# Order of TensorE's products in the column-chunk part of a decoder block: y, combining, transpose and gate products in program order

## The chip, the cores and the metric

The kernel runs on one core of a Trainium2 chip. The metric is the device time of one execution in microseconds. A core has five engines with a queue of instructions each: TensorE (PE in the profile) multiplies matrices into PSUM, VectorE (DVE) and ScalarE (ACT) work on tiles in SBUF and PSUM, GpSimd (POOL) does little here, and SyncE (SP) issues nearly all transfers. Sixteen DMA engines carry these out. An engine takes its instructions in the order of its queue; between engines semaphores order the work.

## The reference

One layer of a decoder block on 256 tokens of width 2048, all in fp32: a recurrent and a convolutional mixer share one input and one output projection; a mixture of 32 experts follows, and a gated embedding:

```
x = x + concat(o_hg, o_sc) @ w_out
hn = rms_norm(x, g_ffn)
x = x + hier_moe(hn, ...)            # one group of 4, two experts of 8; w_gate, w_up, w_down of 32 experts
ple = rms_norm(p @ w_ple, g_ple)
x = x + sigmoid(x @ w_ple_gate) * ple
return rms_norm(x, g_final)
```

An expert computes `(silu(a) * b) @ w_down[e]` with `a = xb @ w_gate[e]` and `b = xb @ w_up[e]`. Its three matrices are 2048x512, 2048x512 and 512x2048, 4 MB each, so 32 experts bring 384 MB through the core, and `w_ple_gate` (2048x2048) 16 MB.

## The kernel before, in words

The tokens are kept as two halves j = 0, 1 of 128 rows. The residual stream is `x1[j]` (128 x 2048). Experts go in eight blocks b = 0..7 of four. Each expert takes up to 32 tokens, so the four experts of a block are put side by side on the array: a product of expert e uses a strip of 32 columns of the array (shown as 128*32), and four experts fill the 128 columns.

After the gate and up products of all blocks (`hT`, the hidden values, transposed), the down products come in two parts. In the first (L1042 to L1060, blocks 0 to 3, `NBR = 4`) whole rows of `w_down` are loaded. In the second, the column-chunk part (L1141 to L1193, blocks 4 to 7), the 2048 output columns are taken in five chunks, `CHUNKS` of 512, 512, 512, 256 and 256 columns; all four blocks are done for one chunk before the next starts. By numbers: chunk 0 to chunk 4. The reason for chunks is that a finished chunk of the residual stream lets the product `x @ w_ple_gate` begin for these rows.

In a chunk, for each block b: four weight pieces (two in the chunks of 256 columns, where a piece holds two experts) are taken from the list of loaded ones; 16 products (4 parts f of the hidden width, 4 experts e) give `ys`, 128 slots x w, in PSUM (L1162); the slots of the weights are refilled, that is, the next piece on the list is issued into them; ScalarE copies `ys` to `yt` (L1171). `combine` (L1150) multiplies with `PwT[b]`, which spreads the slots to the tokens with their weights, and adds into `acc[j]`. It is called one block late: combine(b-1) after y(b), and combine(7) at the end of the chunk.

A fp32 product stands as two instructions in the trace; a gate product (fp32r) and a transpose as one.

When a chunk is done, its gate work becomes a generator, `embedding_gate`, which the next chunk advances by `next(job)`: `residual` adds `acc` to `x1` on VectorE (L1080), transposes the chunk on TensorE (L1087) and splits it to a high and a low part (ScalarE L1089, VectorE L1090). For each of four column groups n, `split_gate` splits the gate weights in the same way (ScalarE L1102, VectorE L1103, into two slots that are used in turn), and `gate_mm` (L1112 to L1114) multiplies, three products for each k and half j: 24 products per n for a chunk of 512, 12 for 256. The sum over chunks, `Gs`, is kept in SBUF (L1137, L1139). In the last chunk `gate_sum` (L1121) puts a part of `Gs` back into PSUM, and after the last combine the gate of chunk 4 itself ends the kernel with the sigmoid, the final norm and the stores.

The generator is advanced twice in the first block of a chunk (`residual` and the first split; then gate group 0 and the next split), once in each other block, and twice in the second block of chunk 4.

Weights come in pieces of 1 MB through SP's queue in one fixed list; in this part for each chunk: the pieces of block 4, half of the gate pieces of the chunk before, block 5, the other half, block 6, block 7. Ten slots are in turn in this part: a piece is issued when the slot ten pieces back is free.

The order of the instructions on an engine is not the order of the Python lines. A scheduler at compile time simulates the program and takes what it believes to be ready; it may move a product of y between gate products, or a combine ahead of a gate group. `tc.issue_after(ins)` gives each instruction of its block an edge behind `ins` on the same engine: it fixes the order and adds no semaphore. Before the change only two places near the end use it in this part (L1196, L1223).

PSUM: four banks `mm` (the accumulators, later the sums of the gate) and four banks `ms` that go round between y, x2T and G.

Of the kernel before, what the change touches and what calls it, by code (L numbers as in the profile page):

```python
# [15 lines left out]
P = 128  # L16
# [10 lines left out]
NB = NE // 4  # L27
CAP = 32
B_PLE = NB - 4
NBR = NB - 4  # L30
# [5 lines left out]
def kernel(ctx, tc, a, out, dbg=None):  # L36
    nc = tc.nc
# [14 lines left out]
    def slot(i, shape, dt=F32, name="t"):  # L52
        return slots.tile(shape, dt, tag=f"s{i}", name=nm(name))

    def tmp4(shape, name="tmp"):
        return tmp.tile(shape, F32, tag="tmp", name=nm(name))

    def bank(shape=(P, 512), name="mm"):
        return psA.tile(list(shape), F32, tag="mm", name=nm(name))

    def misc(shape=(P, 512), name="ms"):
        return psB.tile(list(shape), F32, tag="ms", name=nm(name))

    def f32(t):
        return t.bitcast(F32)

    V, A, G, MM = nc.vector, nc.scalar, nc.gpsimd, nc.tensor.matmul
# [3 lines left out]
    ident = consts[:, 0:P]  # L71
# [81 lines left out]
    state = {"next": 0}  # L153
# [12 lines left out]
    def take():  # L166
        return loaded.pop(0)
# [43 lines left out]
    ps = misc(name="vg")  # L211
# [99 lines left out]
    def refill_slot(s):  # L311
        if want[0] > 0:
            want[0] -= 1
            free.append(s)
        elif state["next"] < limit.get(s, 1 << 30):
            give(s)
# [208 lines left out]
    ps = misc((P, 4, 4), "gf")  # L525
# [104 lines left out]
    x1 = []  # L630
# [136 lines left out]
    ps = misc((P, P), "cntT")  # L767
# [9 lines left out]
    hT, ple = [], []  # L777
# [153 lines left out]
    for b in range(NB):  # L931
# [7 lines left out]
        if b == 0:  # L939
# [3 lines left out]
            hT = [slot(free.pop(0), [P, 2, NB, P], name="hT") for _ in range(2)]  # L943
        if b == B_PLE:
            ple = [slot(free.pop(0), [P, D], name="ple") for _ in range(2)]
            PwT = slot(free.pop(0), [P, NB, T], name="PwT")
# [96 lines left out]
    for b in range(NBR):  # L1043
        ys = [bank(name="y") for _ in range(4)]
        for k in range(4):
            four = [take() for _ in range(4)]
            for n in range(4):
                for e in range(4):
                    q = slice(32 * e, 32 * e + 32)
# [14 lines left out]
    Gs = [slot(xg_slots[j], [P, D], name="G") for j in range(2)]  # L1064
    want[0] += 3
    gate_slots = []

    def accumulator(w):

        if w == 512:  # L1070
            return [bank(name="acc") for _ in range(2)], 1
        t = bank((P, 2, w), "acc")
        return [t[:, j] for j in range(2)], 2

    def residual(c0, w, acc):

        nk = w // P
        cs = slice(c0, c0 + w)
        for j in range(2):
            V.tensor_tensor(x1[j][:, cs], acc[j], x1[j][:, cs], OP.add)  # L1080
        t = slot(xt_slot, [P, 2, 4, T], F32R, name="x2T")
        for k2 in range(0, nk, 2):
            ps = misc((P, 2, T), "x2T")
            for kk in range(2):
                k = c0 // P + k2 + kk
                for j in range(2):
                    state["x2T"] = nc.tensor.transpose(ps[:, kk, j * P:(j + 1) * P], x1[j][:, k * P:(k + 1) * P], ident)  # L1087
            ks = slice(k2, k2 + 2)
            A.copy(t[:, 0, ks], ps)  # L1089
            V.tensor_tensor(t[:, 1, ks], ps, f32(t[:, 0, ks]), OP.subtract)  # L1090
        return t

    def split_gate(n, mine, slots_):

        c = (n % 2) * 512
        part = []
        for i, g in enumerate(mine):
            s = slots_.pop(0)
            slots_.append(s)
            t = slot(s, [P, 2, 2, 512], F32R, name="ghl")  # L1100
            src = g[1][:, :, c:c + 512]
            state["split"] = A.copy(t[:, 0], src)  # L1102
            V.tensor_tensor(t[:, 1], src, f32(t[:, 0]), OP.subtract)  # L1103
            part += [(2 * i + q, t[:, 0, q], t[:, 1, q]) for q in range(2)]
            if n % 2 == 1:
                refill_slot(g[0])
        return part

    def gate_mm(ps, xT, part, j, start):
        ts = slice(j * P, (j + 1) * P)  # L1110
        for i, (k, wh, wl) in enumerate(part):
            MM(ps, xT[:, 0, k, ts], wh, start=start and i == 0, stop=False)  # L1112
            MM(ps, xT[:, 1, k, ts], wh, start=False, stop=False)  # L1113
            state["gate"] = MM(ps, xT[:, 0, k, ts], wl, start=False, stop=i == len(part) - 1)  # L1114

    gb = {}

    def gate_sum(j, n, alloc):

        gb[j, n] = alloc(name="Gf")  # L1120
        MM(gb[j, n], ident, Gs[j][:, n * 512:(n + 1) * 512], start=True, stop=False)  # L1121

    def embedding_gate(c0, w, acc, first):

        xT = residual(c0, w, acc)
        nh = w // (2 * P)
        for n in range(4):
            if n % 2 == 0:
                mine = [take() for _ in range(nh)]
            part = split_gate(n, mine, gate_slots)  # L1130
            yield
            for j in range(2):
                ps = misc(name="G")
                gate_mm(ps, xT, part, j, True)
                g = Gs[j][:, n * 512:(n + 1) * 512]
                if first:
                    A.copy(g, ps)  # L1137
                else:
                    V.tensor_tensor(g, ps, g, OP.add)  # L1139

    job = None  # L1141
    for ci, (c0, w) in enumerate(CHUNKS):
        last = ci == len(CHUNKS) - 1
        acc, shared = accumulator(w)
        ne = 512 // w
        held = []

        def combine(b, yt):
            for j in range(2):
                MM(acc[j], PwT[:, b, j * P:(j + 1) * P], yt[:, :w], start=b == NBR and j % shared == 0,  # L1150
                   stop=b == NB - 1 and (j + 1) % shared == 0)

        late = None
        for b in range(NBR, NB):
            while len(held) < 4:
                s, t = take()
                held += [(s, t[:, q], q == ne - 1) for q in range(ne)]
            ys = misc(name="y")
            for f in range(4):
                for e in range(4):  # L1160
                    q = slice(32 * e, 32 * e + 32)
                    MM(ys[q, :w], hT[f // 2][:, f % 2, b, q], held[e][1][:, f], start=f == 0, stop=f == 3)  # L1162
            for s, t, fin in held[:4]:
                if fin:
                    refill_slot(s)
            held = held[4:]
            if ci == 0 and b == NBR:
                gate_slots += [free.pop(0) for _ in range(2)]
                xt_slot = free.pop(0)
            yt = tmp4([P, 512], "y")  # L1170
            A.copy(yt[:, :w], ys[:, :w])  # L1171
            if late is not None:
                combine(*late)
            late = (b, yt)
            if job is not None:
                for _ in range(2 if b == NBR or last and b == NBR + 1 else 1):
                    next(job, None)
            if last and b == NBR:
                want[0] += 4
            if last and b == NBR + 1:  # L1180
                own = [take() for _ in range(2)]
            if last and b >= NB - 2:
                if b == NB - 2:
                    parts = {}
                    for n in range(3):
                        gate_sum(0, n, bank)
                n = 2 * (b - NB + 2)
                for q in range(n, n + 2):
                    parts[q] = split_gate(q, [own[q // 2]], free)
        combine(*late)  # L1190
        if not last:
            job = embedding_gate(c0, w, acc, ci == 0)


    xT = residual(c0, w, acc)
    with tc.issue_after(state["x2T"].ins):  # L1196
        gate_sum(0, 3, misc)
        gate_sum(1, 0, misc)
# [99 lines left out]
```

## Time and profile before

| | |
|---|---|
| time, median of 3 runs | 1515.95 us (1514.32 to 1516.35) |
| profiled execution, its own time | 1514.15 us |
| its span, first to last instruction | 1512.4 us |
| TensorE busy | 1348.1 us (89%) |
| VectorE, ScalarE busy | 466.7, 340.1 us |
| read from HBM | 502.19 MB |
| mean granted TensorE clock | 0.966 |

The column-chunk part starts at 1261 us of the span and its last combine ends at 1481; the tail after it lasts until 1512.4. A granted clock of 1.00 is 2.4 GHz, 0.50 is 1.2 GHz. The share of the DMA engines is a mean over 16 engines and can stand a little above 1, since packets of one engine overlap. Durations of products include the time until their last result, so products in a row overlap; the distance from one start to the next is what one costs.

### The profile page before, as it was taken

How to read it: one execution, taken by the hardware profiler on the slowest of the kernel's cores; microseconds unless marked ns; L12 is line 12 of the kernel's file. 1: busy time of each engine (PE TensorE's matmuls, PEld its weight loads, DVE VectorE, ACT ScalarE, POOL GpSimd, SP SyncE). 2: the span in 40 equal slices, each digit the busy share in tenths (PEclk: the TensorE clock that was granted, in tenths of full speed). 3: DMA queues.
4: the chain of work that ended last, by engine and by line, in shares of the span. 5: the costliest groups of instructions: out<-in, count | busy, mean ns of one | idle time of the engine just before them, and what ended most of it. 6: DMA issues, size and time to landing. Idle time of an engine off the chain costs nothing. (4 is left out here: it accounts for less than half of the span.)

```text
span 1512.4 us, 19734 instructions
## 1 busy us (share of the span) xinstructions
PE 1348.1 (89%) x8490; PEld 811.4 (54%) x8490; DVE 466.7 (31%) x750; ACT 340.1 (22%) x469; POOL 21.5 (1%) x36
## 2 busy tenths in 40 slices
PE   9999999999999987768688887766699998999995
PEld 9998999999897642324152424211132322344563
DVE  6778756575443100000011221000001111213355
ACT  6665456364431000000001000000010001221223
POOL 1001100000000000000000000000000000000000
PEclk9999999999999999999898999989799999999998
DMA  8755635579556999999999999999999999999971
GB/s 317 259 165 173 222 97 183 168 263 344 174 200 272 399 421 421 421 421 419 423 421 421 421 377 421 421 421 421 421 420 421 422 412 387 393 383 343 368 260 56
DMA packets 140378, 505.64 MB, mean 334 GB/s; under 512 B 12361, under 2 KB 33210, under 8 KB 98814
## 3 DMA queue, kind: packets, MB, share of 16 engines
q1 hardware_dynamic: 139726, 501.74, 85.3%
q0 software_dynamic: 384, 2.36, 0.4%
q8 instruction: 69, 1.13, 0.3%
q10 hardware_dynamic: 176, 0.22, 0.1%
q14 instruction: 23, 0.19, 0.0%
HBM read 502.19 MB, written 2.10 MB: 333 GB/s over the span
## 5 line engine op out<-in xcount | busy, mean ns | idle before, releaser
L856 PE MATMUL uk<-w,xg 128*32 128x512 f32 x1024 | 202.3, 710 | 85.5 <-DMA w<-in_w_up_dram 85.5
L337 PE MATMUL mm<-xh,whl 128*128 128x256 f32 x768 | 218.8, 285 | 0.7 <-ACT xh L259 0.7
L339 PE MATMUL mm<-xh,whl 128*128 128x256 f32 x768 | 217.6, 283 | 0.1
L338 PE MATMUL mm<-xl,whl 128*128 128x256 f32 x768 | 217.4, 283 | 0.3 <-DVE xl L260 0.2
L301 DVE TENSOR_TENSOR whl<-w,whl 128x1024 fp32r<-128x1024 f32 (+1 forms) x146 | 176.0, 1213 | 110.0 <-ACT whl L300 109.5
L300 ACT CAST whl<-w 128x1024 fp32r<-128x1024 f32 (+1 forms) x146 | 150.6, 1036 | 187.5 <-PE mm L339 113.1
L856 PE MATMUL gk<-w,xg 128*32 128x512 f32 x1024 | 161.9, 623 | 31.3 <-DMA w<-in_w_gate_dram 31.3
L856 PEld LDWEIGHTS uk<-w,xg 128*32 128x32 f32 x1024 | 43.7, 126 | 237.7 <-DMA w<-in_w_up_dram 158.9
L337 PEld LDWEIGHTS mm<-xh,whl 128*128 128x128 f32 x768 | 147.1, 192 | 1.5 <-ACT xh L259 0.9
L338 PEld LDWEIGHTS mm<-xl,whl 128*128 128x128 f32 x768 | 147.3, 192 | 0.9 <-DVE xl L260 0.8
L339 PEld LDWEIGHTS mm<-xh,whl 128*128 128x128 f32 x768 | 147.2, 192 | 0.4 <-DVE whl L301 0.3
L1050 PE MATMUL y<-w,hT 128*32 128x512 f32 x512 | 134.6, 604 | 6.4 <-PEq L1019 6.4
L797 PEld LDWEIGHTS xg<-Pg,x 128*128 128x128 f32 x512 | 121.4, 328 | 16.6 <-issue 15.4
L797 PE MATMUL xg<-Pg,x 128*128 128x128 f32 x512 | 125.4, 401 | 0.7 <-DVE Pg L791 0.7
L865 DVE TENSOR_TENSOR sg<-sg,uk 128x512 f32<-128x512 f32 x8 | 5.5, 688 | 389.0 <-PE uk L856 389.0
L856 PEld LDWEIGHTS gk<-w,xg 128*32 128x32 f32 x1024 | 37.9, 113 | 128.5 <-issue 68.3
L1050 PEld LDWEIGHTS y<-w,hT 128*32 128x32 f32 x512 | 37.9, 111 | 100.8 <-issue 96.0
L1162 PE MATMUL y<-w,hT 128*32 128x512 f32 (+1 forms) x640 | 86.6, 511 | 3.7 <-DMA w<-in_w_down_dram 3.7
L870 ACT COPY hT<-hT 128x256 f32<-128x256 f32 x8 | 3.0, 373 | 299.4 <-PE hT L869 299.4
L1040 DVE TENSOR_TENSOR x<-acc,x 128x512 f32<-128x512 f32 x32 | 22.1, 692 | 138.0 <-PE acc L1039 138.0
L800 DVE TENSOR_TENSOR xg<-xg,gfq 128x512 f32<-128x512 f32 x32 | 22.1, 692 | 126.3 <-PE xg L797 126.3
L1103 DVE TENSOR_TENSOR ghl<-w,ghl 128x1024 fp32r<-128x1024 f32 x32 | 38.5, 1222 | 56.5 <-ACT ghl L1102 56.3
(293 smaller groups left out, 1323.7 us busy)
## 6 DMA issues: line engine op xcount, KB each, us to landing
w<-in_w_gate_dram SPq DMA_DIRECT2D x128, 1024.0 KB, 19.8
w<-in_w_up_dram SPq DMA_DIRECT2D x128, 1024.0 KB, 19.8
w<-in_w_down_dram SPq DMA_DIRECT2D x128, 1024.0 KB, 15.4
w<-in_w_in_dram SPq DMA_DIRECT2D x55, 1024.0 KB, 5.3
w<-in_w_out_dram SPq DMA_DIRECT2D x16, 1024.0 KB, 6.6
w<-in_w_ple_gate_dram SPq DMA_DIRECT2D x16, 1024.0 KB, 11.4
xa<-in_x_dram SPq DMA_DIRECT2D x8, 256.0 KB, 4.9
x<-in_x_dram POOLq DMA_DIRECT2D x2, 1024.0 KB, 8.2
```

The source lines that it names most:

```text
L300: state["copy"] = A.copy(wh, wf)
L301: V.tensor_tensor(wl, wf, f32(wh), OP.subtract)
L337: MM(o, wh[:, kk, cs], b_h, start=first, stop=False)
L338: MM(o, wh[:, kk, cs], b_l, start=False, stop=False)
L339: MM(o, wl[:, kk, cs], b_h, start=False, stop=last)
L797: MM(ps[:, kk], x1[j][:, kq * 512 + kk:(kq + 1) * 512:4], Pr[j], start=kk == 0 and j == 0, stop=kk == 3 and j == 1)
L800: state["xg"] = V.tensor_tensor(xg[:, ks], ps, gfq[:, kq].unsqueeze(2).to_broadcast([P, 4, P]), OP.mult)
L856: MM(bk[q], xg[:, k, q], four[e][1][:, kk], start=k == 0, stop=k == KT - 1)
L1040: V.tensor_tensor(x1[j][:, ns], acc, x1[j][:, ns], OP.add)
L1050: MM(ys[n][q], hT[k // 2][:, k % 2, b, q], four[e][1][:, n * 512:(n + 1) * 512], start=k == 0, stop=k == 3)
L1103: V.tensor_tensor(t[:, 1], src, f32(t[:, 0]), OP.subtract)
L1162: MM(ys[q, :w], hT[f // 2][:, f % 2, b, q], held[e][1][:, f], start=f == 0, stop=f == 3)
```

## The change

A helper `seq()` opens `tc.issue_after` behind the last TensorE instruction noted in `state["pe"]`. Every TensorE instruction of the column-chunk part is put in such a block: the four products of one f of a y group, a combine, the transposes of two k, the gate products of one n and j, a gate sum; each block notes its last instruction. So TensorE's queue has them in the order of the Python lines. `embedding_gate` gets a `yield` behind `residual`, and the first block of a chunk advances the generator once more, between f = 1 and f = 2 of its y products. So `residual` of the chunk before is issued in the middle of that y group; the two calls at the end of the block do the first split, and gate group 0 with the next split, as before.

```diff
+    def seq():
+        return tc.issue_after(state["pe"].ins) if "pe" in state else ExitStack()
...
             ps = misc((P, 2, T), "x2T")
-            for kk in range(2):
-                k = c0 // P + k2 + kk
-                for j in range(2):
-                    state["x2T"] = nc.tensor.transpose(ps[:, kk, j * P:(j + 1) * P], x1[j][:, k * P:(k + 1) * P], ident)
+            with seq():
+                for kk in range(2):
+                    k = c0 // P + k2 + kk
+                    for j in range(2):
+                        state["x2T"] = nc.tensor.transpose(ps[:, kk, j * P:(j + 1) * P], x1[j][:, k * P:(k + 1) * P], ident)
+            state["pe"] = state["x2T"]
...
         gb[j, n] = alloc(name="Gf")
-        MM(gb[j, n], ident, Gs[j][:, n * 512:(n + 1) * 512], start=True, stop=False)
+        with seq():
+            state["pe"] = MM(gb[j, n], ident, Gs[j][:, n * 512:(n + 1) * 512], start=True, stop=False)
...
         xT = residual(c0, w, acc)
+        yield
...
-                gate_mm(ps, xT, part, j, True)
+                with seq():
+                    gate_mm(ps, xT, part, j, True)
+                state["pe"] = state["gate"]
...
         def combine(b, yt):
-            for j in range(2):
-                MM(acc[j], PwT[:, b, j * P:(j + 1) * P], yt[:, :w], start=b == NBR and j % shared == 0,
-                   stop=b == NB - 1 and (j + 1) % shared == 0)
+            with seq():
+                for j in range(2):
+                    last_acc = MM(acc[j], PwT[:, b, j * P:(j + 1) * P], yt[:, :w], start=b == NBR and j % shared == 0,
+                                  stop=b == NB - 1 and (j + 1) % shared == 0)
+            state["pe"] = last_acc
...
             for f in range(4):
-                for e in range(4):
-                    q = slice(32 * e, 32 * e + 32)
-                    MM(ys[q, :w], hT[f // 2][:, f % 2, b, q], held[e][1][:, f], start=f == 0, stop=f == 3)
+                if f == 2 and b == NBR and job is not None:
+                    next(job)
+                with seq():
+                    for e in range(4):
+                        q = slice(32 * e, 32 * e + 32)
+                        last_y = MM(ys[q, :w], hT[f // 2][:, f % 2, b, q], held[e][1][:, f], start=f == 0, stop=f == 3)
+                state["pe"] = last_y
```

## Rows read from the trace of the kernel before

**Rows 1.** Busy us of each engine (instructions) by stretch, granted clock, DMA share, GB/s.
```profile
1261.00:1295.60 34.60, 29.04 (x159) 9.04 (x158) 3.53 (x6) 3.42 (x6) 0.00 (x0) 1.00 1.05 388
1295.60:1354.00 58.40, 55.62 (x246) 25.73 (x246) 11.01 (x10) 14.87 (x21) 0.00 (x0) 1.00 1.04 387
1390.00:1396.00 6.00, 5.33 (x35) 1.64 (x33) 2.96 (x3) 1.66 (x3) 0.00 (x0) 1.00 0.39 118
1094.20:1098.20 4.00, 4.00 (x10) 1.67 (x12) 2.25 (x12) 0.00 (x0) 0.00 (x0) 0.50 1.01 418
```

**Rows 2.** Chain that ended last: start, us, what, 1300 to 1341.
```profile
1307.46 0.98 PE y L1162 x2
1308.43 0.43 PE G L1112
1308.86 0.23 PE G L1113
...
1316.54 3.56 PE y L1162 x26
```

**Rows 3.** TensorE in order of time: start, us, line, xcount, idle before and releaser.
```profile
1307.39 1.05 PE L1162 MATMUL y<-w,hT 128*32 128x512 f32 x2
...
1401.56 1.04 PE L1162 MATMUL y<-w,hT 128*32 128x512 f32 x2
...
1416.10 0.50 PE L1112 MATMUL G<-ghl,x2T 128*128 128x512 f32 x1 [0.79 <-ACT ghl L1102]
...
1422.10 0.63 PE L1162 MATMUL y<-w,hT 128*32 128x256 f32 x4
...
1476.24 0.63 PE L1162 MATMUL y<-w,hT 128*32 128x256 f32 x4
```

**Rows 4.** TensorE in order of time: whole groups of each kind.
```profile
1265.63 1.98 PE L1150 MATMUL acc<-y,PwT 128*128 128x512 f32 x4
1267.55 3.64 PE L1162 MATMUL y<-w,hT 128*32 128x512 f32 x32
...
1292.53 0.88 PE L1087 MATMUL x2T<-consts,x 128*128 128x128 f32 x6
...
1449.64 1.93 PE L1162 MATMUL y<-w,hT 128*32 128x256 f32 x32
...
1479.82 1.13 PE L1150 MATMUL acc<-y,PwT 128*128 128x256 f32 x4 [0.47 <-ACT y L1171]
1481.47 0.88 PE L1087 MATMUL x2T<-consts,x 128*128 128x128 f32 x4 [0.52 <-DVE x L1080]
1482.19 1.88 PE L1121 MATMUL Gf<-G,consts 128*128 128x512 f32 x4
```

**Rows 5.** TensorE's waits from 1295 to 1481: us in total, times, longest.
```profile
PE acc L1150 <- ACT y L1171: 7.0, 10, 1.0
```

**Rows 6.** Waits of SP's queue from 1357 to 1400: us in total, times, longest.
```profile
SPq L162 <- PE y L1162: 24.0, 6, 11.7
```

**Rows 7.** The last weight piece: its issue on SP, and its landing.
```profile
L162 SPq DMA_DIRECT2D w<-in_w_down_dram x1: 2883/2883/2883, 1453.6 to 1453.6; - x1
...
DMA to landing us min/median/max: 11.8/11.8/11.8
```

**Rows 8.** The last piece of chunk 2's third block, in the same way.
```profile
L162 SPq DMA_DIRECT2D w<-in_w_down_dram x1: 1501/1501/1501, 1368.4 to 1368.4; - x1
...
DMA to landing us min/median/max: 13.9/13.9/13.9
```

**Rows 9.** ScalarE in order of time, 1413 to 1418.
```profile
1413.75 0.37 ACT L1171 COPY y<-y 128x256 f32<-128x256 f32 x1 [5.16 <-PE y L1162]
...
1414.98 2.02 ACT L1102 CAST ghl<-w 128x1024 fp32r<-128x1024 f32 x2
```

**Rows 10.** The page's groups: count, busy us, mean ns, idle before.
```profile
L1103 DVE TENSOR_TENSOR ghl<-w,ghl 128x1024 fp32r<-128x1024 f32 x32 | 38.5, 1222 | 56.5 <-ACT ghl L1102 56.3
```

**Rows 11.** TensorE in order of time, the first product of the down part.
```profile
1094.18 1.20 PE L1050 MATMUL y<-w,hT 128*32 128x512 f32 x2 [6.39 <-PEq L1019]
```

## The prediction

> **What bounds the kernel now.** I read the busy time by stretch first, then the chain of waits, then TensorE's own instructions in order of time, then its waits, and last the issues and landings of the weight transfers. The stretches of the column-chunk part [rows 1] say two things at once: TensorE is busy for 95% of the time in chunk 1 (55.62 of 58.40 us), and the 16 DMA engines are full (share 1.04). Two resources that both look full call for a look at which of them is really used. The chain [rows 2] runs through TensorE alone, in alternation: gate products (G), then one product of y ("x2": an fp32 product is two instructions) for 0.98 us, then a gate product of 0.43 instead of 0.23 us, and later the rest of that y group in 3.56 us. So a lone product costs 0.98 + 0.20 = 1.18 us. It saves nothing in the rest: 26 instructions take 3.56 us, all 32 take 3.6 [rows 2, 4], as if an incomplete four of products took as long as a full one. "Busy" counts all of this as work.
>
> Between 1296 and 1411 us there are 17 such lone wide products (the first at 1307.39, the last at 1401.56, [rows 3]), so 17 x 1.18 = 20.1 us. In the narrow chunks (256 columns) six pairs of products are split off the same way, of 0.63 us each (first at 1422.10, last at 1476.24); with a switch of 0.2 us that is 6 x 0.8 = 4.8 us. Third, the combining product is put right behind the y group whose copy it needs, and TensorE waits for ScalarE: 10 times, 7.0 us [rows 5]. Together about 32 us of the 185.4 us between 1295.6 and 1481 are order, not work.
>
> **Can it be cashed?** Only as far as the weights arrive. In the first stretch [rows 1] TensorE waits for weights while the engines move 388 GB/s at share 1.05; that is the ceiling for these pieces. From there on the transfers have one hole, 1390 to 1396: share 0.39 instead of 1.05, 3.8 us lost, because the queue's issues waited, up to 11.7 us each, for slots that a late TensorE had not freed [rows 6]. The last piece lands at 1453.6 + 11.8 = 1465.4 [rows 7]; without the hole at 1461.6. The y group that reads it takes 1.9 us and ends at 1479.35, 0.47 before the combine [rows 4], so it starts at 1477.4: TensorE is 12 us behind the transfers at the end. So the change is worth what TensorE can catch up, at most to the transfers.
>
> **The change, part by part.**
> *Each y group in one piece, gates behind it.* Per wide block: y 3.6, combining 1.9 (1265.63 to 1267.55), a gate group of 24 products 24 x 0.23 = 5.5 us [rows 2, 4]: 11 us, and 44 + 1.2 for the eight transposes (0.88 for six) = 45 us a chunk. Its 16 down pieces and 4 gate pieces of 1.05 MB take 21 MB / 387 GB/s = 54 us. So in chunks 1 and 2 TensorE, faster than its weights, will wait for them; the lone products disappear and about 18 us of the gain turn into waits on y. The largest are those of the third block, in front of whose four pieces two gate pieces are loaded: 6 x 2.7 = 16 us of transfer against 11 of work, a wait of 5. The last one is that of chunk 2, whose last piece lands at 1368.4 + 13.9 = 1382.3 [rows 8]. From there TensorE is the limit, in program order:
> chunk 2: y 3.6, combine 1.9, gate 5.5, y 3.6, combine 1.9, gate 5.5, combine 1.9 = 23.9, to 1406.2;
> chunk 3: four y of 1.9 = 7.6, transposes 1.2, four gates of 5.5 = 22.0, four combines of 1.0 (1.13 less its tail) = 4.0, together 34.8, to 1441.0;
> chunk 4: y 7.6, transposes 0.6, 48 gate products 11.0, three gate sums 2.6 (two take 1.88 with the tail), combines 4.0, together 25.8, to 1466.8.
> Ten changes from y's strips to the full array at 0.2 us (0.43 less 0.23, [rows 2]): 2.0, to 1468.8. The last combining product now ends at 1479.82 + 1.13 = 1480.95 [rows 4]. Gain so far 12.1 us. What follows it (residual, 48 gate products, store) is left as it is.
>
> *Combining one block late.* In program order combine(b-1) follows y(b), so its copy is 10 us old and the wait of 0.7 us goes; at the end of a chunk combine(b-1) and a gate group lie between y and its own combine. Only in the last chunk is the gate group gone; there combine(6), 1.0 us, covers a copy of 0.37 us. Nothing is late next. Cost 0.
>
> *Residual and transposes between f = 1 and f = 2 of the next chunk's first y group.* It issues two VectorE adds, four or eight transposes, one or two ScalarE casts and VectorE differences, no transfer, and passes no issue on SP's queue: pieces are taken and refilled in the old order. The half group in front (1.8 us wide, 0.95 narrow) covers the adds, for which TensorE waited 0.52 us behind the last combine of the last chunk (1481.47, [rows 4]). PSUM: four banks go round between y, transposes and gate; the one asked for is four allocations old. I cost it at nothing beyond a break of the group, in the 0.2 above; between 0 and 0.5 us.
>
> *The wait that is added.* Behind the first y group of a chunk nothing is left to combine, and the first gate group now stands directly behind it. It needs ScalarE's split of the gate weights, and ScalarE's rows [rows 9] show that split behind the y copy (1413.75, then 1414.98). Before, TensorE still idled 0.79 us there [rows 3] with a combine of 1.1 us in between. In program order that cover is gone: copy 0.37 and one split 1.05 before the first product, VectorE's half 1.22 [rows 10] before the third, less four products that can run: 1.8 us at most, 0 if ScalarE takes the split first. Behind the waiting product stand all later y groups, and behind them the slots. In chunks 1 and 2 the wait for weights hides it (4 to 5 us before the next y); in chunks 3 and 4 it is on the path. I take 1.5 each, near the row: 3.0 us.
>
> *The clock.* The new waits of about 5 us leave TensorE idle. The only comparable row: after 6.39 us of idle time the granted clock was 0.50 (1.2 GHz) for the 4 us that followed [rows 1, 11]. After the first waits the next one absorbs it; after the one at 1382.3 it is on the path: 0 if the clock holds, 2 us if 4 us run at half speed. I take 0.7.
> The Trainium skill ("TensorE: Matmul & The Clock Gate", section "HAM oscillation — how this bites in real kernels") says that a loop which waits for its weights between groups of products starts every group at the low clock. The trace agrees for the one long wait, and shows 1.00 through the short waits of the first stretch of rows 1; by the rule at its full weight all waits in chunks 1 and 2 would do it, which is the clock rival below.
>
> Sum: 12.1 - 3.0 - 0.7 = 8.4 us. The profiled execution took 1514.15 us (span 1512.4 and 1.75 around it), so 1505.75 by it; the runs' median is 1515.95, 1.8 above it, and 8.4 less gives 1507.5, the forecast.
>
> **Rivals.**
> A, no new wait: the scheduler puts the splits ahead of the copy and the clock holds. 12.1 us, and never more than the last landing allows: 1461.6 + y 1.9 + two combines 2.0 = 1465.5, a gain of 15.4. Time 1500.5 to 1503.9. For it: ScalarE has room (14.87 us busy of 58.40, [rows 1]); against: the order in rows 9.
> B, the clock: every wait for weights in chunks 1 and 2 halves the clock, and work of 4 us or more behind it runs at half speed, with a second fall where the stalls of chunks 3 and 4 add idle time. 2 us at each of three places that nothing absorbs: 8.4 - 6 + 0.7 = 3.1 us gained, 1512.8.
> C, slower: the fixed order makes each gate group wait for its split, not just the first of a chunk. From 1382.3 on stand ten gate groups. If each finds its split behind the copy of the y group in front, less the narrow combine of 1.0 that covers some, it waits 0.37 + 1.05 + 1.22 - 1.0 = 1.64 us: 16.4 us against the 12.1, so 4.3 slower, 1520. It decides from 1.21 us a group. Against it: in program order the split of group n+1 is issued before y(b+1), so y and combine (2.9 us narrow, 5.5 wide) cover it.
> D, no effect: the order edges change little, or the planner had hidden more than the rows show. 1514 to 1517.
>
> **How the numbers follow.** Forecast 54%, A 20%, B 12%, C 8%, D 6%. A measurement of this kernel tells 0.2%, 3.0 us, from no change. Faster: all of the forecast and A, 9 of B's 12, 1 of D: 0.84. Same: the rest of B, 4 of D: 0.07. Slower: C and 1 of D: 0.09. The range has A's floor, 1500, as its low end; the high end takes in B, to 1513. C and D stay outside, 14%, and a little of A.
>
> **What would show it.** Right: no y row of two instructions between gate rows; TensorE's waits of the combining products on ScalarE near 0; waits of y on weights of 12 to 18 us in chunks 1 and 2; the hole at 1390 gone, last landing near 1462; the last combine's end at 1472 +-3. The stalls: first gate group of chunks 3 and 4 waiting 1 to 2 us for ScalarE's split. The clock: below 1.00 around 1382. Wrong: gate groups that wait in the middle of chunks (C), holes in the transfers (then the slots, not TensorE, set the pace), or an end of combining above 1476.

## The result, and the profile after

The changed kernel takes 1502.91 us (median of 4 runs, 1500.68 to 1503.39), the kernel before 1515.62 us beside it (4 runs): ratio 0.9916, 95% interval 0.99 to 0.9931, 12.7 us less. The forecast was 8.4 us less, 1507.5, with a range of 1500 to 1513.

The traced execution took 1500.68 us with a span of 1499.0. Lines have moved: y is now L1177, the combine L1161, the transposes L1092, gate products L1118 to L1120, splits L1108 (ScalarE) and L1109 (VectorE), the y copy L1187, gate sums L1128.

Busy time by stretch, with the columns of [rows 1]; the chunks are cut where they now begin, and two short stretches follow:

```profile
1295.60:1351.00 55.40, 50.81 (x246) 25.72 (x242) 12.09 (x12) 16.01 (x22) 0.00 (x0) 0.97 1.04 391
1351.00:1404.00 53.00, 47.73 (x245) 25.04 (x238) 16.00 (x19) 12.89 (x16) 0.00 (x0) 1.00 1.05 384
1404.00:1440.00 36.00, 35.86 (x250) 25.46 (x249) 17.09 (x21) 11.01 (x15) 0.00 (x0) 1.00 1.08 363
1440.00:1468.00 28.00, 27.14 (x205) 17.15 (x203) 16.58 (x22) 8.74 (x12) 0.00 (x0) 1.00 0.70 243
1390.00:1396.00 6.00, 6.00 (x45) 2.90 (x43) 3.65 (x4) 2.10 (x2) 0.00 (x0) 1.00 1.08 351
1312.00:1314.00 2.00, 2.00 (x16) 0.50 (x12) 0.00 (x0) 0.00 (x0) 0.00 (x0) 0.50 1.01 396
1380.00:1388.00 8.00, 6.34 (x35) 2.51 (x35) 0.00 (x0) 0.59 (x1) 0.00 (x0) 1.00 1.05 386
```

In chunks 1 and 2 TensorE is less busy than before and the transfers stay full; in chunks 3 and 4 it is busy nearly all the time. The hole in the transfers at 1390 (share 0.39 in [rows 1]) is gone. The clock fell to 0.50 once in chunk 1, and held behind the wait at 1382.

TensorE's waits from 1295 to 1468 (us in total, times, longest), which answer to [rows 5]:

```profile
PE y L1177 <- DMA w<-in_w_down_dram: 10.1, 7, 1.7
PE G L1120 <- DVE ghl L1109: 1.4, 4, 0.4
PE x2T L1092 <- DVE x L1084: 0.4, 1, 0.4
```

The waits of the combine on ScalarE are gone; waits for weights stand in their place.

TensorE in order of time around the last of them and at the chunks' ends, to set beside [rows 3, 4]:

```profile
1375.53 1.84 PE L1177 MATMUL y<-w,hT 128*32 128x512 f32 x4
1379.04 1.05 PE L1177 MATMUL y<-w,hT 128*32 128x512 f32 x2 [1.67 <-DMA w<-in_w_down_dram]
1381.75 3.62 PE L1177 MATMUL y<-w,hT 128*32 128x512 f32 x26 [1.66 <-DMA w<-in_w_down_dram]
...
1392.70 3.64 PE L1177 MATMUL y<-w,hT 128*32 128x512 f32 x32
...
1403.58 1.88 PE L1161 MATMUL acc<-y,PwT 128*128 128x512 f32 x4
...
1407.77 1.07 PE L1177 MATMUL y<-w,hT 128*32 128x256 f32 x16
1408.77 0.50 PE L1118 MATMUL G<-ghl,x2T 128*128 128x512 f32 x1
...
1465.54 1.99 PE L1161 MATMUL acc<-y,PwT 128*128 128x256 f32 x8
```

The rows of two instructions that are left are products in front of a piece that has not landed; no gate product stands between them. A whole group takes 3.64 us. The third block of chunk 2 begins at 1375.53, and the 26 instructions that take as long as a whole group start at 1381.75, 6.2 us later. That is what the missing weights cost there; the waits show 3.3 us of it, and the rest counts as busy. The first gate group of chunk 3, at 1408.77, does not wait. The last combine ends at 1467.53, 13.4 us earlier than in [rows 4].

The last weight piece, its issue and landing, as in [rows 7]:

```profile
L162 SPq DMA_DIRECT2D w<-in_w_down_dram x1: 2767/2767/2767, 1449.1 to 1449.1; - x1
...
DMA to landing us min/median/max: 11.7/11.7/11.7
```

It lands at 1460.8 and the last combine ends 6.7 us behind it; before, these were 1465.4 and 15.6 us. What follows the last combine is 31.5 us in both (1499.0 - 1467.5 and 1512.4 - 1480.95).

One part of the 13.5 us between the two traced executions is not the change's. The first product of the down part, as in [rows 11], is 2.2 us earlier already, in a part where both kernels have the same instructions:

```profile
1092.02 5.66 PE L1050 MATMUL y<-w,hT 128*32 128x512 f32 x16 [6.47 <-PEq L1019]
```

Less this start the two traces are 11.3 us apart. The medians, 12.7 us apart (10.5 to 15.2 by the interval), are the better measure of what the change is worth, since they do not hang on one execution.

### The profile page after: what moved, and what is told of

It is laid out like the page before. It is cut to its first block, busy times and chain, and to the rows that moved or that the text cites. A ratio compares the mean times of both kernels' runs of the same rounds, so it can differ in the third digit from the quotient of the medians.

```text
span 1499.0 us, 19727 instructions
## 1 busy us (share of the span) xinstructions
PE 1333.2 (89%) x8490; PEld 811.9 (54%) x8490; DVE 466.1 (31%) x750; ACT 341.1 (23%) x469; POOL 21.9 (1%) x36
## 5 line engine op out<-in xcount | busy, mean ns | idle before, releaser
L856 PE MATMUL uk<-w,xg 128*32 128x512 f32 x1024 | 197.1, 687 | 92.8 <-DMA w<-in_w_up_dram 92.8
L856 PE MATMUL gk<-w,xg 128*32 128x512 f32 x1024 | 165.7, 640 | 23.4 <-DMA w<-in_w_gate_dram 23.4
L1050 PEld LDWEIGHTS y<-w,hT 128*32 128x32 f32 x512 | 37.9, 111 | 100.9 <-issue 96.9
L1177 PE MATMUL y<-w,hT 128*32 128x512 f32 (+1 forms) x640 | 77.0, 534 | 15.0 <-DMA w<-in_w_down_dram 15.0
L1177 PEld LDWEIGHTS y<-w,hT 128*32 128x32 f32 x640 | 21.3, 112 | 64.2 <-issue 30.5
```

The lines of the kernel that those rows point to most:

```text
L856: MM(bk[q], xg[:, k, q], four[e][1][:, kk], start=k == 0, stop=k == KT - 1)
L1050: MM(ys[n][q], hT[k // 2][:, k % 2, b, q], four[e][1][:, n * 512:(n + 1) * 512], start=k == 0, stop=k == 3)
L1177: last_y = MM(ys[q, :w], hT[f // 2][:, f % 2, b, q], held[e][1][:, f], start=f == 0, stop=f == 3)
```

## The experiments

All variants are of the changed kernel, run beside the kernel before (whose medians were 1515.6, 1515.5 and 1515.2 in the first three sets and 1514.8 in the last). A median alone mixes in what an execution lost before the column-chunk part. So the table has a second measure, from each trace: the end of the last combine less the landing of the last piece (its issue plus its time to landing, as above). It is TensorE's own lag behind the transfers, in that one execution; a fall of the clock in it counts too.

| kernel | median us (runs) | ratio to before, 95% | lag us, worked out |
|---|---|---|---|
| before | 1515.62 (4) | 1 | 1480.95 - 1465.4 = 15.6 |
| changed, first runs | 1502.91 (4) | 0.9916 (0.99 to 0.9931) | 1467.5 - 1460.8 = 6.7 |
| changed, again | 1502.85 (5) | 0.9918 (0.9906 to 0.9931) | 1468.1 - 1461.6 = 6.5 |
| order alone | 1503.79 (6) | 0.9921 (0.9909 to 0.9934) | 1471.7 - 1462.6 = 9.1 |
| move alone | 1514.46 (10) | 0.9993 (0.9984 to 1.0002) | 1479.3 - 1464.3 = 15.0 |
| gate products free | 1511.08 (5) | 0.9965 (0.9953 to 0.9978) | 1474.8 - 1461.9 = 12.9 |
| combines free | 1502.51 (5) | 0.9912 (0.9899 to 0.9924) | 1468.8 - 1462.1 = 6.7 |
| one lone product a block | 1506.14 (5) | 0.9937 (0.9924 to 0.9949) | 1474.6 - 1464.0 = 10.6 |
| split behind the copy | 1507.14 (6) | 0.9953 (0.9936 to 0.997) | 1471.7 - 1461.4 = 10.3 |
| 8 KB rows, changed | 1491.51 (4) | 0.9843 (0.9828 to 0.9857) | |
| 8 KB rows, before | 1510.89 (7) | 0.9973 (0.9962 to 0.9984) | |

**The changed kernel again.** No edit.

> The changed kernel once more, beside the variants, as their base: 1502 to 1503.5. Theory (the clock falls behind some of TensorE's waits for weights, and how often differs between executions): the traced execution has stretches at 0.50 only behind waits of more than one us, in chunks 0 to 2, and if one lies behind the wait at 1382 it is some 2 us slower than the 1500.7 traced before. Rival (the executions differ for another reason): same clock rows, other time.

Measured: 1502.85 us (1501.18 to 1505.15). The traced execution took 1501.24 us, with the clock at 0.50 in chunks 0 and 1 only. That fits the theory without testing it; the run with the order alone and the runs with extra products say more.

**The order alone.**

```diff
-                if f == 2 and b == NBR and job is not None:
-                    next(job)
...
         xT = residual(c0, w, acc)
-        yield
```

> The fixed order alone; residual and transposes stay behind the whole first y group of a chunk. Theory (the order of TensorE brings the gain, the move only hides the casts of the transposed chunk): transposes then stand directly in front of gate group 0, which waits for cast 0.59 and difference 0.69, about 1.3 us in each of chunks 3 and 4, hidden by weights in 1 and 2: 1505.5, about 2.6 above the changed kernel. Rival (the move brings most of it): 1511 or more.

Measured: 1503.79 us, 0.9 above the changed kernel, which is less than the two intervals can tell apart; the lag is 2.4 us longer. The move is not where the gain is. Most of that lag is not the move's either. Behind the last wait for weights the granted clock fell in this execution, and the 26 instructions that take 3.62 us at 1381.75 in the changed kernel take 5.32, 1.7 us more:

```profile
1383.73 5.32 PE L1174 MATMUL y<-w,hT 128*32 128x512 f32 x26 [1.66 <-DMA w<-in_w_down_dram]
1384.00:1388.00 4.00, 4.00 (x24) 0.98 (x17) 0.00 (x0) 0.00 (x0) 0.00 (x0) 0.57 1.05 387
```

That leaves 0.7 us, where 2.6 was expected. TensorE's rows of chunk 3 show what the move hides, the cast and the difference of the transposed chunk: 0.46 us here, and 0.90 in chunk 4. It is less than expected: the splits of the gate weights are already done there, and the first cast starts while the later transposes still run:

```profile
1410.91 1.09 PE L1092 MATMUL x2T<-consts,x 128*128 128x128 f32 x8
1412.25 0.50 PE L1118 MATMUL G<-ghl,x2T 128*128 128x512 f32 x1 [0.24 <-ACT x2T L1095]
1412.97 0.50 PE L1119 MATMUL G<-ghl,x2T 128*128 128x512 f32 x1 [0.22 <-DVE x2T L1096]
```

In chunks 1 and 2 of this run the splits are not done ahead. There the split stands behind the y copy, and gate group 0 waits 1.67 and 1.68 us for it, where the waits for weights hide that:

```profile
1358.75 0.50 PE L1118 MATMUL G<-ghl,x2T 128*128 128x512 f32 x1 [1.68 <-ACT ghl L1108]
```

**The move alone.**

```diff
     def seq():
-        return tc.issue_after(state["pe"].ins) if "pe" in state else ExitStack()
+        return ExitStack()
```

> The move of residual into the first y group alone, no fixed order of TensorE. Theory (the order is the gain): the lone products and the waits of combining are all back, 1513 to 1517. Rival (the move brings it): 1505 or less.

Measured: 1514.46 us, within the bound of no change. Its trace has the lone products and the combine's waits back, the latter 7.5 us in 11 from 1295 to 1480. In chunk 3 ScalarE's split stands behind the y copy, as in the kernel before:

```profile
1413.61 0.37 ACT L1187 COPY y<-y 128x256 f32<-128x256 f32 x1 [0.31 <-PE y L1177]
1413.88 2.00 ACT L1108 CAST ghl<-w 128x1024 fp32r<-128x1024 f32 x2
```

**Gate products outside the fixed order.**

```diff
-                with seq():
-                    gate_mm(ps, xT, part, j, True)
-                state["pe"] = state["gate"]
+                gate_mm(ps, xT, part, j, True)
```

> The changed kernel with the gate products left out of the fixed order, so that the scheduler puts them between products of y again (12 lone products in wide chunks, 6 pairs in narrow ones; no combine waits for its copy). Theory (lone products cost 1.18 us wide and 0.8 narrow; those in front of the wait for the weights at 1382 are absorbed by the waits): 2 x 1.18 + 5 x 0.8 = 6.4 us stay, 1509. Rival (the combine's waits or the moved residual were the gain): 1503.

Measured: 1511.08 us, 8.2 above the changed kernel; by the lag 6.2, where 6.4 was expected. Products of chunk 2 and 3 in order of time, gate rows between them left out:

```profile
1391.59 1.05 PE L1175 MATMUL y<-w,hT 128*32 128x512 f32 x2
1393.94 1.04 PE L1175 MATMUL y<-w,hT 128*32 128x512 f32 x2
1398.32 1.04 PE L1175 MATMUL y<-w,hT 128*32 128x512 f32 x2
...
1418.40 0.63 PE L1175 MATMUL y<-w,hT 128*32 128x256 f32 x4
1421.00 1.92 PE L1175 MATMUL y<-w,hT 128*32 128x256 f32 x28
```

The lone products are back, with none of them waiting for weights. The combines do not wait for their copies, and still some two thirds of the gain are lost (8.2 of 12.7 us). That 6.2 and 6.4 agree is partly luck, since the terms differ. With the landings set equal, chunk 3 begins 1.4 us later than in the changed kernel (1407.83 against 1405.38, less 1.1 of later landing), where 2.4 was said for two wide products; TensorE no longer waits for weights behind 1296, and four lone wide products start behind 1382. Chunks 3 and 4 take 4.85 us longer (67.00 against 62.15). Of it 1.46 is a wait that the expectation left out, that of gate group 0 of chunk 3 for ScalarE's split, and the rest, 3.4, falls to the five broken narrow groups, for which 4.0 was said:

```profile
1412.38 0.50 PE L1118 MATMUL G<-ghl,x2T 128*128 128x512 f32 x1 [1.46 <-ACT ghl L1108]
```

So this run takes away two things, whole y groups and the early split; the runs with one lone product and with the late split take them apart.

**Combines outside the fixed order.** In `combine` the `with seq()` and the note in `state["pe"]` are left out.

> The changed kernel with the combining products left out of the fixed order. Theory (whole y groups are what counts; the scheduler puts the combines behind gate products, where the copy is ready, and breaks one y group of chunk 2 twice): 1503 to 1505. Rival (the waits of combining on ScalarE, 7.0 us before, were the larger part): 1507 or more.

Measured: 1502.51 us, as the changed kernel. With gates and y fixed, the scheduler puts the combines behind gate products, and one wait of 0.2 us on the y copy is left. That the time is the same hides two changes that cancel. The scheduler breaks the y group of chunk 2 behind the last wait twice, which costs about 2 us, and it does a combine of 1.9 us in front of that wait (1377.24) that the changed kernel does behind it (1385.30):

```profile
1377.24 1.88 PE L1160 MATMUL acc<-y,PwT 128*128 128x512 f32 x4
1392.53 1.05 PE L1175 MATMUL y<-w,hT 128*32 128x512 f32 x4
```

In sum the fixed place of the combines brings nothing here.

**One lone product a block.** Each y product also has a `seq()` block of its own here, and in the runs with extra products below, where the changed kernel has one for the four products of one f.

```diff
-                with seq():
-                    for e in range(4):
-                        q = slice(32 * e, 32 * e + 32)
+                for e in range(4):
+                    q = slice(32 * e, 32 * e + 32)
+                    with seq():
                         last_y = MM(...)
-                state["pe"] = last_y
+                    state["pe"] = last_y
+                    if f == 0 and e == 0 and late is not None:
+                        combine(*late)
+                        late = None
```

> The changed kernel with one product of each y group of blocks 5 to 7 put in front of the combine, the other 15 behind it: one lone product a block, same work, same transfers. Theory (a lone product takes the time of four and saves nothing): behind the wait at 1382 stand one wide and six narrow ones, 1.18 + 6 x 0.76 = 5.7 us, 1508.6. Rival (broken groups cost no time, the gain came from gates standing behind y): 1503.

Measured: 1506.14 us, 3.3 above the changed kernel; lag 3.9 longer. A narrow block of chunk 3:

```profile
1416.65 0.62 PE L1177 MATMUL y<-w,hT 128*32 128x256 f32 x2
1417.20 1.13 PE L1161 MATMUL acc<-y,PwT 128*128 128x256 f32 x4
1418.27 1.93 PE L1177 MATMUL y<-w,hT 128*32 128x256 f32 x30
1425.76 0.62 PE L1177 MATMUL y<-w,hT 128*32 128x256 f32 x2
```

From 1416.65 to 1425.76 is 9.11 us a block; in the changed kernel the same block takes 8.40 (y groups from 1414.45 to 1422.85): 0.71 for a lone narrow product, 0.76 expected. 15 products behind it take 1.93 us, as 16 do. The one wide product makes the last block of chunk 2 12.00 us long (1393.96 to 1405.96) against 10.88 (1392.70 to 1403.58), 1.1 for 1.18 expected. So the price stands. The sum was set wrong: in this kernel the combine in front of the last wait for weights (1.9 us) is done before that wait, where the changed kernel does it behind; 5.7 - 1.9 = 3.8 us is what should have been expected, and 0.48 more for the last combine, which here waits for its y copy.

**ScalarE's first split behind the y copy.**

```diff
-            state["split"] = A.copy(t[:, 0], src)
+            with tc.issue_after(state["yt"].ins) if n == 0 else ExitStack():
+                state["split"] = A.copy(t[:, 0], src)
...
-            A.copy(yt[:, :w], ys[:, :w])
+            state["yt"] = A.copy(yt[:, :w], ys[:, :w])
```

> The changed kernel with ScalarE's first split of each chunk's gate weights ordered behind the y copy, as it stood in the kernel before. Theory (the wait that was forecast did not come because the splits were taken ahead): gate group 0 of chunks 3 and 4 now waits up to 1.8 us each, 3 to 3.6 in all, hidden by weights in chunks 1 and 2: 1506. Rival (other work covers the split): 1503.

Measured: 1507.14 us, 4.3 above the changed kernel; lag 3.6 longer. In chunk 3 ScalarE and TensorE read so:

```profile
1409.37 0.37 ACT L1188 COPY y<-y 128x256 f32<-128x256 f32 x1 [0.42 <-PE y L1178]
1409.63 2.00 ACT L1109 CAST ghl<-w 128x1024 fp32r<-128x1024 f32 x2
```

```profile
1408.20 1.07 PE L1178 MATMUL y<-w,hT 128*32 128x256 f32 x16
1410.74 0.50 PE L1119 MATMUL G<-ghl,x2T 128*128 128x512 f32 x1 [1.46 <-ACT ghl L1109]
```

This is the wait that was forecast, with the price that was forecast: 1.46 us in chunk 3 and again in chunk 4, where 1.5 each was taken, and 0.52 more in each for VectorE's half. In the changed kernel ScalarE's order is another one in chunk 3, and likewise in chunk 4, which is why the wait did not come:

```profile
1402.41 1.05 ACT L1108 CAST ghl<-w 128x1024 fp32r<-128x1024 f32 x1 [5.34 <-PE G L1120]
1403.79 1.04 ACT L1108 CAST ghl<-w 128x1024 fp32r<-128x1024 f32 x1 [0.32 <-PE G L1120]
1407.44 1.07 ACT L1095 CAST x2T<-x2T 128x512 fp32r<-128x512 f32 x2 [2.60 <-PE x2T L1092]
1408.93 0.37 ACT L1187 COPY y<-y 128x256 f32<-128x256 f32 x1 [0.42 <-PE y L1177]
```

Here the splits run as soon as the last gate group of the chunk before frees their slots, 6.5 us ahead of the copy. In each run with the gate products in the fixed order and the split left free, at least the first split of chunks 3 and 4 stands ahead of the copy in the trace. With the move alone and with the gate products free it stands behind the copy in chunk 3. Why the scheduler chooses so is not shown.

**Down weights in rows of 8 KB**, for the changed kernel and the one before. Other numbers are multiplied, so the output is not the reference's; bytes, pieces and products are the same.

```diff
-                pieces.append(a["w_down"][0, e:e + ne, :, c0:c0 + w].rearrange("e (k p) n -> p e k n", p=P))
+                pieces.append(a["w_down"][0, e].rearrange("(p k) n -> p k n", k=4)[:, ci % 4]
+                              .rearrange("p (e k n) -> p e k n", e=ne, k=4))
```

> The changed kernel with the down weights of the column-chunk part read from other places, in rows of 8 KB in place of 2 and 1 KB: same bytes and products, other numbers. Theory (to 1382 the transfers at 388 GB/s set the pace): at the 421 GB/s of the part before, the pieces of chunks 0 to 2 land some 8% earlier, 9 to 11 us by then, and TensorE's 85 us from there on are as before: 1492 to 1494. Rival (TensorE's order is the bound all along): 1501 or more.

> The kernel before with the down weights of the column-chunk part read in rows of 8 KB: same bytes and products, other numbers. Theory (from 1296 on TensorE's order, not the transfers, was the bound before): only chunk 0, which waits for weights, gains, 8% of 57 us of transfers issued from 1238 to 1296, 4.5 us: 1511. Rival (the transfers bound the kernel before as they do the changed one): 11 us as there, 1504 to 1505.

Measured: 1491.51 us, 11.3 less than the changed kernel, and 1510.89, 4.4 less than the kernel before beside it (1515.24), where 4.5 was expected. The stretch of chunk 1 in the changed kernel, then in the one before:

```profile
1295.00:1340.00 45.00, 40.81 (x204) 20.35 (x203) 11.09 (x10) 14.58 (x20) 0.00 (x0) 1.00 1.02 419
```

```profile
1290.00:1350.00 60.00, 56.51 (x247) 25.60 (x246) 12.29 (x12) 15.80 (x22) 0.00 (x0) 1.00 0.98 400
```

Quicker transfers (419 for 391 GB/s) are worth 11 us where TensorE can follow them, and little where its order holds it back: there they only leave holes, share 0.98. So the bound of chunks 1 and 2 was TensorE's order before the change, and is the transfers after it. In chunks 3 and 4 it is TensorE in both.

**Extra products in the waits**, three runs to test the clock. In the first one product of 512 columns, in the second two, stand behind each of the first three y products of four groups; in the third one product stands in each of two places. The lines of the three runs are shown together:

```diff
+                    if f == 0 and e < 3 and ci in (1, 2) and b in (NBR + 1, NBR + 2):   # fill1, fill2 (two products)
+                    if f == 0 and e in (1, 2) and ci == 2 and b == NBR + 2:             # fill_last
+                        if e == 0:                                                      # fill_last: e == 1
+                            clk = misc(name="clk")
+                        with seq():
+                            state["pe"] = MM(clk, ident, PwT[:, 0:2].rearrange("p b t -> p (b t)"), start=True, stop=True)
```

> The changed kernel with one extra product of 512 columns (0.86 us, its result unused) behind each of the first three products of the y groups of the second and third blocks in chunks 1 and 2, where TensorE waits 1.65 us for each next piece. Theory (the executions of the changed kernel above 1500.7 are those in which the clock falls behind the wait at 1382): no stretch at 0.50 after 1300, and a median of 1500.7 to 1501.5 in place of 1502.9. Rival (the clock is not what makes them differ): 1502.9, or slower by what the products add, up to 1.5.

> The same with two extra products in each place, 1.72 us, as long as the wait itself. Theory of the clock: no stretch at 0.50 after 1300 either; each group may start up to 0.3 us late: 1500.7 to 1502. Rival: 1503 to 1504.

> The changed kernel with one extra product (about 1 us with the break, result unused) in each of the two waits of 1.67 us that the third block of chunk 2 has, the last ones before TensorE becomes the bound; nothing else. The two fit into the 3.3 us of waiting there. Theory (the executions above 1500.7 are those in which the clock falls behind these waits): none at 0.50 behind 1380, median 1500.7 to 1501.6. Rival (the spread has another cause): 1502.9, the extra products hidden in the waits.

Measured: 1508.41 (ratio 0.9959, 0.9945 to 0.9973), 1518.83 (1.0023, 1.0012 to 1.0033) and 1503.06 us (0.9917, 0.9904 to 0.9931). The first two miss both expected times and say nothing on the clock. No stretch behind 1300 is at 0.50, as expected, but there is not a wait at each of the three places, and hardly a wait is left. TensorE's waits for weights from 1295 on fell from 10.1 us to 0.8 in the first, and then each place, a lone product and an extra one, cost its full 2 us, as here in chunk 1:

```profile
1307.74 1.05 PE L1177 MATMUL y<-w,hT 128*32 128x512 f32 x2
1308.71 1.12 PE L1184 MATMUL clk<-PwT,consts 128*128 128x512 f32 x2
1309.77 1.04 PE L1177 MATMUL y<-w,hT 128*32 128x512 f32 x2
```

TensorE is late again in that run, and the transfers have a hole again, share 0.53 from 1388 to 1394.

The third does test the theory, for the last two waits. Its extra products fit into them; the waits shrink from 1.67 to 0.6 us, and the granted clock stays at 1.00:

```profile
1381.64 1.05 PE L1177 MATMUL y<-w,hT 128*32 128x512 f32 x2 [0.61 <-DMA w<-in_w_down_dram]
1382.61 1.13 PE L1184 MATMUL clk<-PwT,consts 128*128 128x512 f32 x2
1384.34 3.62 PE L1177 MATMUL y<-w,hT 128*32 128x512 f32 x26 [0.60 <-DMA w<-in_w_down_dram]
```

```profile
1376.00:1390.00 14.00, 12.79 (x56) 5.03 (x55) 3.65 (x4) 2.69 (x3) 0.00 (x0) 1.00 1.05 386
```

Still the traced execution took 1503.28 us, 2.6 more than the changed kernel's, and the median did not fall. So a fall of the clock behind these waits is not what makes most executions of the changed kernel slower than 1500.7, though it can happen there, as the run with the order alone shows. What differs in this trace lies earlier: its first product of the down part starts at 1094.06, not at 1092.02, and its last piece lands at 1463.1, not at 1460.8; its lag, 7.0 us, is nearly the same. The traced executions line up by that landing: 1460.8 with 1500.68 us, 1461.6 with 1501.24, 1463.1 with 1503.28, and with the combines free, at the same lag, 1462.1 with 1502.02. The start alone does not order them: with the combines free it is 1094.99. What delays the landing by a few us in some executions was not tried, and for the executions without a trace all of this stays an inference. The clock elsewhere in the program is not cleared by it: of the nine executions of the changed kernel, the three from 1500.7 to 1501.2 us have a mean granted clock of 0.965 to 0.969, the six from 1502.8 to 1505.2 one of 0.960 to 0.963. Whether the lower clock makes them slow, or longer waits lower the clock, is not shown.

## Why the prediction was right, and where its size was off

- **What bounds, and the ceiling.** Right. Lone products cost what was said: 1.1 us for a wide one and 0.71 for a narrow one in the run with one a block, where 1.18 and 0.8 stand in the prediction. The gain is capped by the transfers: last landing 1460.8 (1461.6 said), hole gone, TensorE waiting in chunks 1 and 2, and 11.3 us more to be had from quicker transfers, of which the kernel before could use only 4.4.
- **The walk through the chunks.** Right within 1.3 us at each mark: resumed at 1381.75 (1382.3 said), the combines of chunk 2 done at 1405.4 (1406.2), the last combine at 1467.5 (1468.8 without the two surcharges). The marks were taken from an execution whose down part began 2.2 us later; the length of the walk does not hang on that, and it was 85.8 us where 86.5 was said. By program order there are twelve changes from y's strips to the full array behind 1382.3, not ten, since the two broken first groups have two each; that is 0.4 us.
- **The waits for weights.** Right in place. As waits, 12 to 18 us with 5 for the largest was said, and 10.1 us in pieces of at most 1.7 was measured. But the list has only the idle part: from the first product of a group to its last 26 instructions, the four waiting groups of chunks 1 and 2 lose 4.3, 3.3, 2.4 and 6.2 us (1306.78 to 1311.07, 1323.69 to 1326.99, 1362.24 to 1364.59, 1375.53 to 1381.75), 16 us in all. What is not idle in it are incomplete fours, which count as busy.
- **The combine's wait.** Gone, as said; but the fixed place of the combines is not needed for it, as the run with the combines free shows.
- **The move.** Costed at nothing, and no more than a small gain shows: 0.9 us by the medians, inside their intervals, and 0.7 by the lag when the 1.7 us of the lower clock are taken out. The casts of the transposed chunk, which it covers, were left out of the sum.
- **"The wait that is added", 3.0 us.** This is the step that failed. Its price was right (3.6 us by the lag with the split behind the copy), its condition was not: ScalarE's order was read from the kernel before and taken to hold after. With TensorE's order fixed, the splits of chunks 3 and 4 came ahead of the copy, and the first gate groups did not wait for ScalarE. Rival A named this, at 20%; it is what happened: 12.1 us by A's sum, 12.7 measured. So the signs that rested on the wait failed too: no stall of 1 to 2 us, and an end of the combines at 1467.5, outside 1472 +-3. That 1502.9 lies in the stated range owes to the low end that was set by rival A.
- **"The clock", 0.7 us.** Nothing of it is in the traced total: in both traces of the changed kernel the clock fell in chunks 0 and 1, where waits for weights absorb it, and held behind 1382. As a chance it was well put. With the order alone, behind the same two waits of 1.67 us, the clock fell to 0.57 for 4 us and cost 1.7, where 2 was said for that case.
- **Rivals B, C and D** did not come: no clock loss that counts, waits of gate groups on splits of 1.4 us in all, those in chunks 1 and 2, and an effect four times the bound of no change.

## What to carry to other kernels

In this kernel a product on a strip of the array that stands alone between full-width products cost as much as four side by side or more (1.18 us against 3.64 / 4 = 0.91), and the profile calls it busy: look at the order of the products and price the gaps between starts, not the busy share. Before a gain on one engine is promised, ask what the transfers would allow, and walk from the last wait for data to the end. The order of the other engines is not a constant of the change: where the scheduler is free, a wait read from the old order is a bound, not the likeliest value.

## What the runs showed of the hardware that was not expected

- With all 16 engines full, the bytes moved a second went with the length of a row in HBM: 418 to 420 GB/s with rows of 8 KB, 384 to 391 in the chunks where most rows have 2 KB, 363 in chunk 3, where most have 1 KB. In the runs with 8 KB the places read changed along with the rows.
- Behind waits for weights of at most 1.7 us, with about 1 us of work between them, the granted clock fell to 0.50 at some places (1312 to 1314 in the changed kernel) and held at others (1380 to 1388). Behind the same two waits, with the order alone, it fell to 0.57 from 1384 to 1388.
- Executions of kernels with the same instructions up to there reach the down part between 1091.4 and 1098.1 us (the first with the move alone, the last with one lone product a block). The time followed the last landing of a weight piece, and only loosely this start.
